# A hybrid attention and mixture-of-experts layer: its first projection summed in PSUM by eighths of the channels

## The chip, the cores and the metric

One core of a Trainium2 chip. The metric is the device time of one execution in microseconds (us), median of several runs. The program has some 27,500 instructions on five engines: PE (TensorE; PEld is its weight load), DVE (VectorE), ACT (ScalarE), POOL (GpSimd) and SP (SyncE, which issues nearly all DMAs).

## What is computed

256 tokens of 2048 channels go through one transformer layer in fp32. Only its beginning matters here: a normalized input is scaled and shifted by vectors that come from the conditioning vector `c`, and then multiplied by a wide matrix whose columns are the queries, keys and values of an attention, the inputs of a gated delta rule (`qb, kb, vb`, and its gate `zb`), and further gates.

```python
mod = (jax.nn.silu(c) @ w_ada + b_ada)[:, None, :]
sh1, sc1, g1, sh2, sc2, g2 = jnp.split(mod, 6, axis=-1)
u = layer_norm(x) * (1.0 + sc1) + sh1
hcat = u @ w_in
qa, ka, va, qb, kb, vb, zb, b_logit, a_logit, ga_logit, gb_logit = jnp.split(hcat, split_points, axis=-1)
oa = swa_sink_attention(qa, ka, va, swa_sinks)
...
merged = jax.nn.sigmoid(ga_logit) * (oa @ w_proj_a) + jax.nn.sigmoid(gb_logit) * (ob @ w_proj_b)
x = layer_norm(DEEPNORM_ALPHA * x + g1 * (merged @ w_out), ln1_g, ln1_b)
```

After that come a second scale and shift, a router and 32 experts.

## The kernel before, in words

**Data.** Channels lie on the 128 partitions: `xT` is the normalized input turned, 16 blocks `k` of 128 channels by 256 tokens. Weights come from memory in tiles of 1 MB (128x2048), one DMA on SP's queue each, into a rotating pool of four (`wp`, `wload`, L75). fp32 products are made from three reduced-precision ones: the weight tile is split by halves of 1024 columns into `wh` (cast on ACT, L275) and `wl` (the rest, DVE, L276), `u` into `uh` and `ul` (L176, L177), and `mm3` (L279) issues `wh*uh`, `wh*ul`, `wl*uh` (L280 to L282). One half of a weight tile is a **job**: 8 blocks of 128x128, so 24 products of 256 columns on PE.

**First stage.** Before `u` exists, its scale and shift must be computed from 32 tiles of `w_a01`, four for each of eight groups: quarter `q` of the channels, first scale (`i` = 1), then shift (0). In `first_mods` each tile gives four matmuls (L192) that stand side by side in 32 columns of PE each, into the bank `fa`; after four tiles ACT copies the bank (`fr`, L199), PE turns it by four transposes (`fc`, L169), DVE reduces it to four columns of scale or shift (L170, L171), and after the shift four blocks of `xT` become `u`, `uh`, `ul` (L175 to L177). I call this the turn of a quarter.

As soon as a quarter of `u` is there, its share of 20 column blocks (8 of queries, 2 of keys, 2 of values, 8 of `z`) is computed: `quarter` (L312) appends 10 jobs per quarter (`w_kq`, 5 tiles), each job giving two column blocks over four channel blocks in one PSUM bank `wq`. The first quarter's result is copied to SBUF by ACT (L334), those of the other three are added to it by DVE (L336). `run(few(mods, 8), QCH, ...)` weaves the scale-and-shift steps of the next quarter between the jobs.

**Main stream.** `pieces` appends jobs for the other columns: one tile of `w_in` is one column block over all 16 channel blocks (two jobs), summed in one bank `ws`. `run(chain, per, adas)` emits the jobs in order and puts between them `per` steps per job of a chain (a generator) and `adas` half tiles per job of the later modulation vectors (`ada_steps`, a DVE multiply-add per half tile, L220). The constants `PER` and `ADA` hold these rates for five stretches. The first stretch has the 12 blocks of `conv_todo(0)` (24 jobs) with the chain `gates`, `attn_v`, `attn`, `z_silu`; what is left of the chain when the jobs end is emitted behind them. Then come `conv_todo(1)` with the delta rule `gdn(0)`, the projections with `gdn(1)`, the output projection, and the experts.

**Order.** A scheduler fixes one static order for each engine from the program's order and the dependences; SP's queue is in order too. `sml` and `cmx`, constants that the gates need, are loaded behind the first stage (L801 to L803).

Of the kernel before, what the change touches and what calls it, by code (L numbers as in the profile page):

```python
# [9 lines left out]
F32 = mybir.dt.float32  # L10
# [6 lines left out]
P = 128  # L17
D = 2048
# [48 lines left out]
def tile_block(ctx: ExitStack, tc: tile.TileContext, A: dict, out: bass.AP, dbg=None, upto=99):  # L67
# [63 lines left out]
    SC.activation(csil, craw[:, 0:KT], AF.Silu)  # L131
    crep = gd.tile([P, KT, 32], F32, name="crep")
# [24 lines left out]
    def early_room():  # L157

        a = r1.tile([P, 1024 + 7 * 512], F32, tag="G1", name="wx0")
        b = r2.tile([P, KT, S], F32, tag="X1", name="wx1").rearrange("p k s -> p (k s)")  # L160
        return [t[:, 2048 * j:2048 * j + 2048] for t in (a, b) for j in range(2)]

    def first_mods():

        def use(i, q, mr):
            dst = (sh1c, sc1c)[i][:, 4 * q:4 * q + 4]
            p = pg(f"fc{i}{q}")
            for m in range(4):
                T.transpose(p[:, m * P:(m + 1) * P], mr[:, m * P:(m + 1) * P], ident)  # L169
            V.tensor_reduce(dst, p.rearrange("p (m j r) -> p m j r", m=4, j=4)[:, :, :, 0], axis=AX.X, op=ADD)  # L170
            V.scalar_tensor_tensor(dst, dst, float(i), craw[:, KT * (i + 1) + 4 * q:KT * (i + 1) + 4 * q + 4],  # L171
                                   op0=ADD, op1=ADD)
            if i == 0:
                for k in range(4 * q, 4 * q + 4):
                    V.tensor_scalar(xT[:, k, :], xT[:, k, :], sc1c[:, k:k + 1], sh1c[:, k:k + 1], op0=MUL, op1=ADD)  # L175
                    SC.copy(uh[:, k, :], xT[:, k, :])  # L176
                    V.tensor_tensor(ul[:, k, :], xT[:, k, :], uh[:, k, :].bitcast(F32), op=SUB)  # L177

        late = []
        room = early_room()  # L180
        for q in range(4):
            for i in (1, 0):
                pa = pg(f"fa{i}{q}")
                for t in range(4):
                    src = A["w_a01"][(4 * i + q) * 4 + t]
                    if room:
                        w = room.pop(0)
                        nc.sync.dma_start(w, src)
                    else:
                        w = wload(src)  # L190
                    for k in range(4):
                        T.matmul(pa[32 * k:32 * k + 32, :], crep[:, 4 * t + k, :], w[:, 512 * k:512 * k + 512],  # L192
                                 start=(t == 0), stop=(t == 3))
                    if late and t == LT[1 - i]:
                        use(*late.pop())
                    if t < 3:
                        yield
                mr = rb.tile([P, 512], F32, tag="mr", name=f"fr{i}{q}")
                SC.copy(mr, pa)  # L199
                if i == 0 and LT[0] < 0:  # L200
                    use(i, q, mr)
                else:
                    late.append((i, q, mr))
                yield
        if late:
            use(*late.pop())
        yield
# [44 lines left out]
    sh1c = gd.tile([P, KT], F32, name="sh1c")  # L252
    sc1c = gd.tile([P, KT], F32, name="sc1c")
# [4 lines left out]
    mods = first_mods()  # L258
    for _ in range(FM):
        next(mods)  # L260
    for t in range(NT):
        x0 = xx[:, t, :]
        mu, rs = ln_stats(x0, f"a{t}")
        V.tensor_scalar(x0, x0, mu, rs, op0=SUB, op1=MUL)
        for kq in range(4):
            p = pg(f"xt{t}{kq}")
# [45 lines left out]
    def quarter(q, dsts):  # L312

        for t in range(len(dsts) // 4):
            st = {}

            def prep(hf, t=t, st=st):
                if hf == 0:
                    st["w"] = wload(A["w_kq"][q * TQ + t])
                return split(st["w"][:, hf * 1024:(hf + 1) * 1024])  # L320

            def fin(sp, hf, t=t):
                h, lo = sp
                p = ps_w.tile([P, 512], F32, tag="ws", name=f"wq{q}{t}{hf}")
                for m in range(2):
                    for k in range(4):
                        kk = slice(k * 256 + m * P, k * 256 + m * P + P)
                        mm3(p[:, m * S:(m + 1) * S], (h[:, kk], lo[:, kk]), (uh[:, 4 * q + k, :], ul[:, 4 * q + k, :]),
                            k == 0, k == 3)
                        if k % 2 and m + k < 4:  # L330
                            yield
                dst = dsts[4 * t + 2 * hf].rearrange("p m s -> p (m s)")
                if q == 0:
                    SC.copy(dst, p)  # L334
                else:
                    V.tensor_tensor(dst, dst, p, op=ADD)  # L336

            for hf in range(2):
                jobs.append((lambda hf=hf, prep=prep: prep(hf), lambda sp, hf=hf, fin=fin: fin(sp, hf)))
# [439 lines left out]
    def few(it, n):  # L779
        for _ in range(n):  # L780
            next(it, None)
            yield

    a0 = r2.tile([P, KT, S], F32, tag="X1", name="a0")
# [7 lines left out]
    dsts = [a0[:, i:i + 2, :] for i in range(11)] + [None] + [szT[:, i:i + 2, :] for i in range(7)] + [None]  # L792
    for _ in range(8 - FM + (LT[0] >= 0)):
        next(mods)
    for q in range(4):
        quarter(q, dsts)
    for q in range(3):
        run(few(mods, 8), QCH, split_at=2 * TQ)
    for _ in mods:
        pass  # L800
    for dst, n in ((sml, "small"), (cmx, "cmx")):  # L801
        V.tensor_copy(dst[:, 0:1], sh1c[:, 0:1])
        nc.sync.dma_start(dst, A[n])  # L803
    pieces(conv_todo(0))
    run(None, split_at=2 * TQ)
# [681 lines left out]
def pack(inp):  # L1487
# [6 lines left out]
    a01 = ada[:, :2 * D].reshape(4, 4, P, 2, 4, 512)  # L1494
    r["w_a01"] = a01.transpose(3, 4, 0, 2, 1, 5).reshape(32, P, D)
# [15 lines left out]
    n = 4 * TQ  # L1511
    r["w_kq"] = w[:, cols[:n * P]].reshape(4, 4, P, TQ, 2, 256).transpose(0, 3, 2, 4, 1, 5).reshape(n, P, D)
# [52 lines left out]
```

## Time and profile before

| | |
|---|---|
| median of 3 runs | 1822.61 us (1822.32 to 1824.35) |
| the profiled execution, its own time | 1820.14 us |
| its span, first to last instruction | 1818.2 us |
| mean granted clock of TensorE, of full speed | 0.985 |
| busy over the span: PE, DVE, ACT | 95%, 49%, 28% |
| DMA | 628.59 MB, mean 346 GB/s |

The profile gives for each group of instructions its line, engine, output and inputs, count, busy time and mean duration, and the idle time of the engine just before it with what ended it. A matmul of fp32 data has two records in the trace (two passes). A busy PE is not PE at its peak, since matmuls overlap: the pace is read from starts, or from a stretch's time over its count.

### The profile page before, as it was taken

The page shows a single profiled execution, that of the slowest core. Times are in us where ns is not written, and L with a number is a line of the kernel's source. Part 1 is how long each engine was busy: PE and PEld are TensorE (multiplying, and loading weights), DVE is VectorE, ACT ScalarE, POOL GpSimd, SP SyncE. Part 2 cuts the span into 40 slices and gives each one's busy share as a digit, 9 for nine tenths or more (in the row PEclk, how much of TensorE's full clock was granted, in tenths as well). Part 3 has the DMA queues.
Part 4 walks back from the last instruction along what each step waited for, and adds up shares of the span by engine and source line. Part 5 has one row for each costly group of instructions (what it writes and reads, how often), then busy time and mean ns, then how long its engine had stood idle before and what let it go on. Part 6 is the DMA issues. An engine that isn't in the chain of part 4 may idle for free. (4 is left out here: it accounts for less than half of the span.)

```text
span 1818.2 us, 27495 instructions
## 1 busy us (share of the span) xinstructions
PE 1724.2 (95%) x11518; PEld 1108.4 (61%) x11518; DVE 899.9 (49%) x1463; ACT 516.7 (28%) x957; POOL 45.2 (2%) x49
## 2 busy tenths in 40 slices
PE   5999998999999999998999999999999999999995
PEld 3778987898999999885434443444434444343331
DVE  3345897888878878667123321232123322232026
ACT  3423698336333544435101110011101110011101
POOL 1000000203000000000000000000000000000000
PEclk9999999999999999998999999999999999999998
DMA  9887566465778688978999999999999999999995
GB/s 365 326 320 305 216 240 224 169 242 217 265 288 297 241 302 303 373 283 325 368 380 421 420 420 421 421 420 420 420 421 420 420 421 420 420 420 421 401 423 231
DMA packets 87289, 628.59 MB, mean 346 GB/s; under 512 B 9829, under 2 KB 9829, under 8 KB 11253
## 3 DMA queue, kind: packets, MB, share of 16 engines
q1 hardware_dynamic: 86832, 626.43, 86.4%
q8 instruction: 92, 1.51, 0.3%
q10 hardware_dynamic: 328, 0.36, 0.1%
q14 instruction: 37, 0.30, 0.0%
HBM read 624.65 MB, written 2.10 MB: 345 GB/s over the span
## 5 line engine op out<-in xcount | busy, mean ns | idle before, releaser
L275 ACT CAST wh<-w 128x1024 fp32r<-128x1024 f32 x216 | 226.0, 1049 | 323.4 <-PE ws L281 115.9
L276 DVE TENSOR_TENSOR wl<-w,wh 128x1024 fp32r<-128x1024 f32 x216 | 266.0, 1232 | 77.1 <-PE mx L281 22.8
L1223 PE MATMUL pg<-w,XT 128*64 128x512 f32 x1024 | 277.8, 598 | 3.9 <-DMA w<-in_w_gu 2.9
L1223 PE MATMUL pu<-w,XT 128*64 128x512 f32 x1024 | 274.6, 592 | 0.0
L280 PE MATMUL ws<-uh,wh 128*128 128x256 f32 x896 | 259.8, 290 | 1.1 <-ACT wh L275 1.1
L282 PE MATMUL ws<-uh,wl 128*128 128x256 f32 x896 | 254.6, 284 | 1.9 <-DVE wl L276 1.6
L281 PE MATMUL ws<-ul,wh 128*128 128x256 f32 x896 | 253.9, 283 | 0.0
L1261 PE MATMUL pd<-w,hT 128*64 128x512 f32 x1016 | 234.1, 599 | 0.8 <-DVE hT L1238 0.8
L1230 DVE TENSOR_TENSOR hs<-hs,pu 128x512 f32<-128x512 f32 x16 | 11.0, 688 | 429.0 <-PE pu L1223 429.0
L280 PEld LDWEIGHTS ws<-uh,wh 128*128 128x128 f32 x896 | 169.7, 189 | 11.3 <-issue 7.8
L282 PEld LDWEIGHTS ws<-uh,wl 128*128 128x128 f32 x896 | 169.9, 190 | 3.8 <-DVE wl L276 2.9
L281 PEld LDWEIGHTS ws<-ul,wh 128*128 128x128 f32 x896 | 169.9, 190 | 1.0 <-issue 0.8
L1223 PEld LDWEIGHTS pu<-w,XT 128*64 128x64 f32 x1024 | 77.6, 137 | 146.2 <-issue 146.2
L220 DVE SCALAR_TENSOR_TENSOR acc<-w,csil,acc 128x1024 f32<-128x1024 f32 x128 | 163.1, 1290 | 6.3 <-DMA w<-in_w_ada 6.2
L1223 PEld LDWEIGHTS pg<-w,XT 128*64 128x64 f32 x1024 | 72.5, 136 | 133.9 <-issue 113.1
L1202 PEld LDWEIGHTS xg<-G,xh 128*128 128x128 f32 x1024 | 120.3, 193 | 41.0 <-issue 25.8
L1261 PEld LDWEIGHTS pd<-w,hT 128*64 128x64 f32 x1016 | 66.4, 136 | 124.1 <-issue 110.3
L1202 PE MATMUL xg<-G,xh 128*128 128x128 f32 x1024 | 131.7, 283 | 6.7 <-DVE x L1278 3.5
L1229 ACT ACTIVATE hs<-pg 128x512 f32<-128x512 f32 x16 | 9.6, 597 | 438.9 <-PE pg L1223 438.9
L370 ACT CAST dh<-pd 128x512 fp32r<-128x512 f32 x64 | 37.5, 586 | 281.4 <-DVE pd L1264 161.1
L1264 DVE SCALAR_TENSOR_TENSOR pd<-pd,wsl,g2b 128x512 f32<-128x512 f32 x64 | 48.5, 758 | 103.7 <-PE pd L1261 103.7
L280 PE MATMUL wq<-uh,wh 128*128 128x256 f32 x320 | 93.1, 294 | 5.1 <-ACT uh L176 2.7
(374 smaller groups left out, 2264.4 us busy)
## 6 DMA issues: line engine op xcount, KB each, us to landing
w<-in_w_gu SPq DMA_DIRECT2D x256, 1024.0 KB, 19.8
w<-in_w_dn SPq DMA_DIRECT2D x127, 1024.0 KB, 19.8
w<-in_w_ada SPq DMA_DIRECT2D x64, 1024.0 KB, 5.1
w<-in_w_in SPq DMA_DIRECT2D x56, 1024.0 KB, 4.8
w<-in_w_a SPq DMA_DIRECT2D x28, 1024.0 KB, 6.7
w<-in_w_kq SPq DMA_DIRECT2D x20, 1024.0 KB, 7.0
w<-in_w_pab SPq DMA_DIRECT2D x16, 1024.0 KB, 4.9
w<-in_w_out SPq DMA_DIRECT2D x16, 1024.0 KB, 6.1
```

The lines of the kernel that those rows point to most:

```text
L220: V.scalar_tensor_tensor(acc[:, hc], w[:, hc], csil[:, k:k + 1], acc[:, hc], op0=MUL, op1=ADD)
L275: SC.copy(h, w)
L276: V.tensor_tensor(lo, w, h.bitcast(F32), op=SUB)
L280: T.matmul(p, a[0], b[0], start=first, stop=False)
L281: T.matmul(p, a[0], b[1], start=False, stop=False)
L282: T.matmul(p, a[1], b[0], start=False, stop=last)
L370: SC.copy(h, src)
L1202: T.matmul(p[:, k * P:(k + 1) * P], xh[t][:, (4 * kq + k) * P:(4 * kq + k + 1) * P], Gs[t].bitcast(F32), start=(t == 0), stop=(t == NT - 1))
L1223: T.matmul(dst[64 * e:64 * e + 64, :], XT[:, k, 64 * e:64 * e + 64], we[:, e * 1024 + hv * 512:e * 1024 + hv * 512 + 512], start=(k == 0), ...
L1230: V.tensor_tensor(hs, hs, pup, op=MUL)
L1261: T.matmul(pd[64 * e:64 * e + 64, :], hT[:, f, 64 * e:64 * e + 64], we[:, (2 * (f % 2) + e) * 512:(2 * (f % 2) + e + 1) * 512], start=(f = ...
L1264: V.scalar_tensor_tensor(pd, pd, ws, g2b[:, cs], op0=MUL, op1=MUL)
```

## The change

The first stage goes by eighths of the channels instead of quarters, and covers 12 column blocks (queries, keys, values) instead of 20. For an eighth, scale and shift (two channel blocks each) lie in one bank, so four tiles of `w_a01` and one turn give both. The 12 column blocks have their sums in six PSUM banks for the whole stage (`acc`, two blocks to a bank); the banks are first written by one matmul of zeros each, every product then adds, and each bank is copied out once at the end (three by ACT, three by DVE). The jobs of the stage are 24 (three per eighth), and the steps of the next eighth are written between them by hand. The loads go through ten places (two halves each of three buffers that are needed later, and the four of `wp`), where before four such places were used once each. The 8 blocks of `z` become 16 jobs of the main stream, ahead of `conv_todo(0)`, so that this stretch has 40 jobs. `PER` and `ADA` are set anew. The PSUM pools of the main stream are opened after the first stage, with waits tile by tile. The packing of weights on the host follows.

```diff
-PER = (1.66, 1.55, 0.85, 2.0)
-ADA = (0.9, 0.9, 1.05, 0.63, 0.09)
+FQ = 12
+PER = (1.0, 1.55, 0.85, 2.0)
+ADA = (0.8, 0.9, 0.95, 0.6, 0.09)
...
+    ps_f = fps.enter_context(tc.tile_pool(name="ps_f", bufs=2, space=PSUM))
+    ps_q = fps.enter_context(tc.tile_pool(name="ps_q", bufs=FQ // 2, space=PSUM))
...
+    def stage_buffers():
+
+        g = r1.tile([P, 1024 + 7 * 512], F32, tag="G1", name="wx0")
+        a = r2.tile([P, KT, S], F32, tag="X1", name="wx1").rearrange("p k s -> p (k s)")
+        most = [t[:, 2048 * j:2048 * j + 2048] for t in (g, a) for j in range(2)] + [None] * 4
+        yield from most
+        x2 = r2.tile([P, KT, S], F32, tag="X2", name="wx2").rearrange("p k s -> p (k s)")
+        while True:
+            yield from [x2[:, 0:2048], x2[:, 2048:4096]] + most
...
+    def mod_rows(e, t):
+
+        if t == 0:
+            fa[e] = ps_f.tile([P, 512], F32, tag="f", name=f"fa{e}")
+        w = sload(A["w_a01"][4 * e + t])
+        for k in range(4):
+            T.matmul(fa[e][32 * k:32 * k + 32, :], crep[:, 4 * t + k, :], w[:, 512 * k:512 * k + 512],
+                     start=(t == 0), stop=(t == 3))
+        if t == 3:
+            mr = rb.tile([P, 512], F32, tag="mr", name=f"fr{e}")
+            SC.copy(mr, fa[e])
+            fa[e] = mr
...
+    def mod_turn(e):
+
+        mr = fa.pop(e)
+        p = ps_f.tile([P, 512], F32, tag="f", name=f"fc{e}")
+        for m in range(4):
+            T.transpose(p[:, m * P:(m + 1) * P], mr[:, m * P:(m + 1) * P], ident)
+        dst = modc[:, :, 2 * e:2 * e + 2]
+        V.tensor_reduce(dst, p.rearrange("p (i m j r) -> p i m j r", i=2, m=2, j=4)[:, :, :, :, 0], axis=AX.X, op=ADD)
+        V.tensor_tensor(dst, dst, craw[:, KT:].rearrange("p (i k) -> p i k", i=2)[:, :, 2 * e:2 * e + 2], op=ADD)
+        for k in range(2 * e, 2 * e + 2):
+            V.tensor_scalar(xT[:, k, :], xT[:, k, :], sc1c[:, k:k + 1], sh1c[:, k:k + 1], op0=MUL, op1=ADD)
+            SC.copy(uh[:, k, :], xT[:, k, :])
+            V.tensor_tensor(ul[:, k, :], xT[:, k, :], uh[:, k, :].bitcast(F32), op=SUB)
...
+    def by_eighths():
+
+        acc = [ps_q.tile([P, 512], F32, tag="q", name=f"wq{j}") for j in range(FQ // 2)]
+        for p in acc:
+            T.matmul(p, zero, zero[:, 0:1].to_broadcast([P, 512]), start=True, stop=False)
...
+        mod_turn(0)
+        sp = prep(0)
+        for n in range(24):
+            e, b = n // 3 + 1, n % 3
+            if b < 2 and e < 8:
+                mod_rows(e, 2 * b)
+                mod_rows(e, 2 * b + 1)
+            cur, sp = sp, (prep(n + 1) if n < 23 else None)
+            for i, _ in enumerate(products(n, cur)):
+                if b == 1 and i == 1 and e < 8:
+                    mod_turn(e)
...
-    for q in range(4):
-        quarter(q, dsts)
-    for q in range(3):
-        run(few(mods, 8), QCH, split_at=2 * TQ)
...
+    pieces([(FQ + m, lambda ps, m=m: SC.copy(szT[:, m, :], ps)) for m in range(8)])
     pieces(conv_todo(0))
-    run(None, split_at=2 * TQ)
     ch = seq(gates(), attn_v(), attn(), z_silu())
     run(ch, PER[0], ADA[0])
```

Three places show how the built programs' order moves. First PE at the start of the stage, from the turned input (`xt`) to the first products `wq`; `fa` are the scale-and-shift matmuls, `fc` the transposes of a turn. Before:

```order
L268 MATMUL xt_185<-cst,xx 128x128 x4
L192 MATMUL fa_110<-wx_109,crep 32x512 x8
L192 MATMUL fa_212<-w,crep 32x512 x4
L169 MATMUL fc_219<-cst,fr_210 128x128 x4
L192 MATMUL fa_212<-w,crep 32x512 x12
L169 MATMUL fc_246<-cst,fr_244 128x128 x4
L280 MATMUL wq_275<-uh,wh 128x256
```

And with the change:

```order
L263 MATMUL xt_196<-cst,xx 128x128 x4
L311 MATMUL wq_209<-zero 128x512
L311 MATMUL wq_210<-zero 128x512
L186 MATMUL fa_107<-wx_109,crep 32x512 x4
L311 MATMUL wq_211<-zero 128x512
L311 MATMUL wq_212<-zero 128x512
L311 MATMUL wq_213<-zero 128x512
L311 MATMUL wq_214<-zero 128x512
L198 MATMUL fc_221<-cst,fr_130 128x128 x4
L186 MATMUL fa_240<-w,crep 32x512 x4
L275 MATMUL wq_209<-uh,wh 128x256
```

The first products stood behind eight tiles of `w_a01` and two turns; now they stand behind five tiles, six matmuls of zeros and one turn, four of the zeros between the last tile and the turn.

Then PE at a later turn, `fa` being the last tiles of the group. Before (the second quarter):

```order
L282 MATMUL wq_602<-uh,wl 128x256
L192 MATMUL fa_507<-w,crep 32x512 x8
L169 MATMUL fc_642<-cst,fr_640 128x128 x4
L280 MATMUL wq_665<-uh,wh 128x256
L280 MATMUL wq_697<-uh,wh 128x256
L281 MATMUL wq_665<-ul,wh 128x256
```

With the change (the fourth eighth; `wq_209` is the bank that the next eighth's first products write):

```order
L186 MATMUL fa_489<-wx_287,crep 32x512 x4
L277 MATMUL wq_212<-uh,wl 128x256
L186 MATMUL fa_489<-wx_287,crep 32x512 x4
L198 MATMUL fc_559<-cst,fr_540 128x128 x4
L275 MATMUL wq_213<-uh,wh 128x256
...
L277 MATMUL wq_214<-uh,wl 128x256
L186 MATMUL fa_612<-wx_108,crep 32x512 x4
L275 MATMUL wq_209<-uh,wh 128x256
```

Before, the products behind a turn were those of the new quarter; now 24 products of the old eighth (`wq_213`, `wq_214`) stand between a turn and the first product that needs its result. In four of the seven later turns the last tile stands right before the transposes, as here; in three it stands seven products earlier.

Last, SP's queue at the end of the stage. Before:

```order
L77 DMA w<-in_w_a 128x2048 x2
L803 DMA sml<-in_small 128x641
L803 DMA cmx<-in_cmx 128x1104
L77 DMA w<-in_w_kq 128x2048 x4
L77 DMA w<-in_w_in 128x2048 x2
```

With the change (`wx` are the added places, `w` the four of the pool):

```order
L74 DMA w<-in_w_kq 128x2048
L171 DMA wx_287<-in_w_a 128x2048 x2
L171 DMA wx_108<-in_w_a 128x2048 x2
L171 DMA wx_109<-in_w_kq 128x2048 x2
L799 DMA sml<-in_small 128x641
L799 DMA cmx<-in_cmx 128x1104
L74 DMA w<-in_w_in 128x2048 x2
```

The last six tiles of the stage need no place of the pool, so the first tiles for `z` stand right behind the constants.

## Rows read from the trace of the kernel before

**Rows 1.** Busy time by stretch (us from the start; x is the count).

```profile
core 0: us, PE busy (x) PEld busy (x) DVE busy (x) ACT busy (x) POOL busy (x), PEclk, DMA share, GB/s
22.00:28.00 6.00, 3.68 (x28) 0.79 (x27) 0.34 (x2) 0.28 (x1) 0.00 (x0) 1.00 1.00 418
28.00:34.00 6.00, 1.72 (x12) 0.58 (x12) 2.08 (x9) 1.88 (x4) 0.00 (x0) 0.94 1.01 418
34.00:40.00 6.00, 5.42 (x23) 5.13 (x24) 3.46 (x7) 2.88 (x6) 0.00 (x0) 0.50 0.94 360
...
34.00:193.60 159.60, 153.60 (x1203) 126.89 (x1204) 80.58 (x113) 58.24 (x77) 0.00 (x0) 0.97 0.80 306
193.60:291.70 98.10, 94.23 (x752) 86.08 (x751) 89.69 (x168) 83.30 (x204) 0.91 (x3) 1.00 0.63 230
291.70:327.50 35.80, 30.29 (x276) 26.82 (x274) 27.41 (x39) 29.64 (x84) 6.26 (x4) 0.90 0.57 212
...
640.00:680.00 40.00, 40.00 (x339) 40.00 (x338) 33.17 (x38) 17.62 (x23) 0.00 (x0) 1.00 0.83 304
820.00:830.00 10.00, 10.00 (x46) 8.29 (x45) 9.58 (x9) 3.16 (x3) 0.00 (x0) 1.00 0.77 281
120.00:140.00 20.00, 19.92 (x143) 16.47 (x144) 9.24 (x14) 6.04 (x8) 0.00 (x0) 0.91 0.72 278
...
70.00:80.00 10.00, 7.91 (x59) 5.48 (x59) 5.17 (x11) 5.92 (x10) 0.00 (x0) 1.00 0.86 342
```

**Rows 2.** Groups of PE's instructions from 34 to 193.6 us.

```profile
line engine op names shapes xcount | busy us, mean ns | idle before us <-releasers
L280 PE MATMUL wq<-uh,wh 128*128 128x256 f32 x320 | 93.1, 294 | 5.1 <-ACT uh L176 2.7 <-ACT wh L275 2.4
...
L192 PE MATMUL fa<-w,crep 128*32 128x512 f32 x192 | 25.4, 604 | 0.5 <-DMA w<-in_w_a 0.5
L169 PE MATMUL fc<-cst,fr 128*128 128x128 f32 x24 | 3.9, 286 | 2.1 <-ACT fr L199 2.1
L392 PE MATMUL ba<-xT,sml 128*32 128x256 f32 x26 | 2.1, 387 | 0.0
```

**Rows 3.** Timeline of the start (start, duration, what; idle before).

```profile
19.70 1.92 PE L192 MATMUL fa<-wx,crep 128*32 128x512 f32 x16
...
22.90 0.66 PE L169 MATMUL fc<-cst,fr 128*128 128x128 f32 x4
...
24.29 1.06 PE L192 MATMUL fa<-w,crep 128*32 128x512 f32 x8 [0.74 <-DMA w<-in_w_a]
...
29.26 1.07 PE L192 MATMUL fa<-w,crep 128*32 128x512 f32 x8 [1.42 <-DMA w<-in_w_a]
...
31.78 0.17 DVE L170 TENSOR_REDUCE sh1c<-fc 128x4 f32<-128x16 f32 x1 [7.82 <-PE fc L169]
...
32.71 0.40 ACT L176 CAST uh<-xT 128x256 fp32r<-128x256 f32 x1 [1.67 <-DVE xT L175]
33.02 1.04 ACT L275 CAST wh<-w 128x1024 fp32r<-128x1024 f32 x1
...
34.11 0.58 PE L280 MATMUL wq<-uh,wh 128*128 128x256 f32 x1 [2.37 <-ACT wh L275]
```

**Rows 4.** Timeline of the second quarter's turn on PE.

```profile
76.09 0.66 PE L169 MATMUL fc<-cst,fr 128*128 128x128 f32 x4 [0.70 <-ACT fr L199]
78.10 0.51 PE L280 MATMUL wq<-uh,wh 128*128 128x256 f32 x2 [1.35 <-ACT uh L176]
```

**Rows 5.** Instructions that read the bank `wq` (duration min/median/max, first and last start).

```profile
L336 DVE TENSOR_TENSOR a<-a,wq x18: 686/689/690, 82.5 to 182.4; 128x512 f32<-128x512 f32 x18
L336 DVE TENSOR_TENSOR szT<-szT,wq x12: 680/687/691, 105.4 to 194.4; 128x512 f32<-128x512 f32 x12
```

**Rows 6.** What PE waited for, 180 to 340 us (total, times, longest).

```profile
PE pb L749 <- ACT PT L743: 3.5, 2, 3.3
...
PE ws L282 <- DVE wl L276: 1.6, 3, 0.8
```

More of the change, by code (lines that the diff above doesn't have):

```diff
@@ L131, in tile_block @@
     SC.activation(csil, craw[:, 0:KT], AF.Silu)
+    zero = gd.tile([P, P], F32, name="zero")
+    G.memset(zero, 0.0)
     crep = gd.tile([P, KT, 32], F32, name="crep")
@@ L155, in ada_tile @@
         return wload(A["w_ada"][k * P:(k + 1) * P, (i - 2) * D:(i - 1) * D])
[L157 to L180, printed above, removed]
-        for q in range(4):
[L182 to L207, printed above, removed]
@@ new lines, in sload @@
+    def sload(src):
+        w = next(room)
+        if w is None:
+            return wload(src)
+        nc.sync.dma_start(w, src)
+        return w
+    modc = gd.tile([P, 2, KT], F32, name="modc")
+    sh1c, sc1c = modc[:, 0, :], modc[:, 1, :]
+    V.tensor_scalar(craw[:, 2 * KT:], craw[:, 2 * KT:], 1.0, None, op0=ADD)
+    fa = {}
+    def mod_rows(e, t):
[9 more added lines that the diff above has]
+            fa[e] = mr
@@ L257, in tile_block @@
     nc.sync.dma_start(xx[:, 1, :], A["x"][P:2 * P, :])
-    mods = first_mods()
-    for _ in range(FM):
-        next(mods)
+    for t in range(4):
+        mod_rows(0, t)
     for t in range(NT):
@@ L265, in tile_block @@
         for kq in range(4):
-            p = pg(f"xt{t}{kq}")
+            p = ps_q.tile([P, 512], F32, tag="q", name=f"xt{t}{kq}")
             for k in range(4):
@@ L310, in pieces @@
                 jobs.append((lambda hf=hf, prep=prep: prep(hf), lambda sp, hf=hf, fin=fin: fin(sp, hf)))
[L312 to L339, printed above, removed]
@@ new lines, in by_eighths, with prep, products @@
+    def by_eighths():
+        acc = [ps_q.tile([P, 512], F32, tag="q", name=f"wq{j}") for j in range(FQ // 2)]
+        for p in acc:
+            T.matmul(p, zero, zero[:, 0:1].to_broadcast([P, 512]), start=True, stop=False)
+        ld = {}
+        def prep(n):
+            if n % 2 == 0:
+                ld["w"] = sload(A["w_kq"][n // 2])
+            return split(ld["w"][:, (n % 2) * 1024:(n % 2 + 1) * 1024])
+        def products(n, sp):
+            h, lo = sp
+            e, b = n // 3, n % 3
+            for pc in range(4):
+                m = 4 * b + pc
+                for k in range(2):
+                    kk = slice(k * 512 + pc * P, k * 512 + pc * P + P)
+                    mm3(acc[m // 2][:, (m % 2) * S:(m % 2 + 1) * S], (h[:, kk], lo[:, kk]),
+                        (uh[:, 2 * e + k, :], ul[:, 2 * e + k, :]), False, (e, k, m % 2) == (7, 1, 1))
+                if pc < 3:
+                    yield
+        mod_turn(0)
[9 more added lines that the diff above has]
+                    mod_turn(e)
+        dst = r2.tile([P, KT, S], F32, tag="X1", name="a0")
+        for j, p in enumerate(acc):
+            d = dst[:, 2 * j:2 * j + 2, :].rearrange("p m s -> p (m s)")
+            if j % 2:
+                V.tensor_copy(d, p)
+            else:
+                SC.copy(d, p)
+        return dst
@@ L777, in seq @@
             yield from x
[L779 to L784, printed above, removed]
+    a0 = by_eighths()
     at["q"], at["k"], at["v"] = a0[:, 0:8, :], a0[:, 8:10, :], a0[:, 12:14, :]
@@ L803, in tile_block @@
         nc.sync.dma_start(dst, A[n])
+    fps.close()
+    pps = ExitStack()
+    ps_w = pps.enter_context(tc.tile_pool(name="ps_w", bufs=2, space=PSUM, reuse_waits="tile"))
+    ps_a = pps.enter_context(tc.tile_pool(name="ps_a", bufs=1, space=PSUM, reuse_waits="tile"))
+    ps_g = pps.enter_context(tc.tile_pool(name="ps_g", bufs=5, space=PSUM, reuse_waits="tile"))
+    pieces([(FQ + m, lambda ps, m=m: SC.copy(szT[:, m, :], ps)) for m in range(8)])
     pieces(conv_todo(0))
-    run(None, split_at=2 * TQ)
     ch = seq(gates(), attn_v(), attn(), z_silu())
```

30 lines of the change are left out of this document (8 added, 22 removed).

## The prediction

> **What bounds the kernel now.** I read the busy time by stretch first, to see which engine each stage leans on. From 34.0 to 193.6 us, the products of the first stage, PE is busy 153.6 of 159.6 us, DVE 80.6, ACT 58.2, and the DMA engines at 0.80 of their time [rows 1]. So PE sets the pace there, and work taken off DVE or ACT buys nothing by itself. What does PE do with the time? Its pace with nothing in the way is read where PE, at the full clock, runs little but products: 339 in 40 us, 118 ns each, so a job of 24 products is 2.83 us [rows 1]. The 960 products of the stage are then 113.3 us. The tiles of the next scale and shift add 25.4, the transposes 3.9, the gates' first matmuls 2.1 [rows 2]: 144.7. The other 14.9 us are lost, and the columns on the right say where: waits for `uh`, `wh` and `fr` [rows 2], which stand at the turns of the quarters (0.70 before the transposes, 1.35 behind them [rows 4]), and stretches at a lower clock, 0.50 of full speed from 34 to 40 us and a mean of 0.91 from 120 to 140 [rows 1].
>
> Then the start. Until 34.1 us not one product runs. The timeline shows PE reading one tile of scale and shift every 2.49 us (from 24.29 to 29.26, two steps), each wait ended by a DMA [rows 3], while the DMA engines are full (1.00 and 1.01, 418 GB/s [rows 1]). So the start is bound by the loads that stand ahead of the first product: two of the input and eight of `w_a01`.
>
> Last, the stretch behind the stage, where the attention runs beside 24 jobs: all three engines are nearly full from 193.6 to 291.7 (PE 94.2, DVE 89.7, ACT 83.3 of 98.1), and in the tail PE idles 5.5 of 35.8 us at a mean clock of 0.90 [rows 1].
>
> **The change part by part.** I count to one place that both kernels have: all 40 jobs of queries, keys, values and `z` done. Before, that is 193.6 us.
>
> *The start.* The fourth tile's matmuls end at 19.70 + 1.92 = 21.6 as before, since six loads stand ahead in both. Behind them come four matmuls of zeros. The trace has none; two tiles, each with the same 512 columns in two passes, take 1.92, so 0.96 each [rows 3], 3.8 together, which I take because PE is at the full clock from 22 on [rows 1]; at half of it they would be 7.7, and at nothing the turn could come 3.8 earlier. The copy `fr` hides behind them. Transposes 0.66, then from DVE's reduction to the end of the first `uh` 32.71 + 0.40 - 31.78 = 1.33 [rows 3]. The first product comes at 21.6 + 3.8 + 0.66 + 1.33 = 27.4 instead of 34.1. Before, it waited for `wh` instead, whose cast stood behind `uh` on ACT [rows 3]; now the cast stands ahead.
>
> *The stage.* 576 products at 118 ns: 68.0. 28 tiles at 25.4 / 24 = 1.06: 29.7. Seven transposes at 0.66: 4.6. In four of the seven turns the last tile stands right before the transposes, so the wait for `fr` stays, 0.70 each: 2.8. The wait of 1.35 behind a turn should mostly go, since 24 products (2.83 us) of the old eighth stand there: `uh` needs 1.33 of it. But the second block's `ul` queues behind a cast of `wh` (1.04) and its DVE partner, so I keep 0.5 a turn (between 0 and 1.35): 3.5. Sum 108.6, so the stage ends at 136.0.
>
> Could the loads hold it up? The tile read at 29.26 is the tenth load of the queue. The last but one of the 46 loads of the stage is then there at 29.26 + 35 x 2.49 = 116.4, and its cast (1.04) and four jobs (11.3) end at 128.8. That is the floor of the stage; per eighth the loads need 5.5 x 2.49 = 13.7 us against PE's (108.6 - 8.5) / 7 = 14.3. With ten places they can run ahead by 25 us; nothing on SP's queue waits for a place that is not long free.
>
> *`z` in the main stream.* 384 products at 118 ns are 45.3; their copies on ACT and casts lie beside. The gates' 2.1 us move behind the stage. The place is reached at 136.0 + 45.3 + 2.1 = 183.4 instead of 193.6: **10.2 us gained**.
>
> *DVE and ACT.* 30 additions of 0.69 [rows 5], 20.6 us of DVE, go; six copies come. Cost and gain nothing, as DVE idles half of that stage [rows 1]; without that cover it would be worth up to 20. The end copies are hidden too, since `z` sums in other banks.
>
> *The attention's stretch.* The same chain, 40 steps at 1.0 over 40 jobs instead of 39.8 at 1.66 over 24, so the tail of steps behind the jobs stays the same. DVE gets 16 splits (1.2 each) and 10.4 more half tiles (1.3 each), 33 us, over 45 more: 123 of 143, less crowded than before. What PE can get back is its idle 3.9 us, and at most some of the tail's 5.5. Of the named waits in there 1.6 are for `wl` and 3.5 for the attention's own copies [rows 6]. I take **4 us**, between 0 and 9.
>
> *Later.* `ADA`, over the jobs of the five stretches, brings 40 x 0.8 + 24 x 0.9 + 48 x 0.95 + 48 x 0.6 + 32 x 0.09 = 130.9 of 132 half tiles, where 24 x 0.9 + 24 x 0.9 + 48 x 1.05 + 48 x 0.63 + 32 x 0.09 = 126.7 came before: four fewer at the end, some 5 us of DVE, where PE is full (10.0 of 10 from 820 on [rows 1]). Nothing, at most 2. The experts follow unchanged.
>
> Sum: 14.2 us off the profiled execution's own 1820.1 gives 1805.9. The median of the runs shown is 2.5 above that execution, so I predict **1808.5**.
>
> **The rivals.** *The loads set the pace and PE loses nothing beside them:* the stage ends at its floor, 128.8, 7.2 earlier: 1801.3. For it: 13.7 against 14.3 us an eighth is close, and PE could run on at the full clock. Against: the waits at the turns are in PE's own order.
>
> *The turns cost as much as before:* seven at 0.70 + 1.35 instead of 6.3 in all are 8.1 more, and with the zeros at half clock 3.9 more still: 1816.6 to 1820.5. For it: a turn's chain through ACT, PE and DVE is as long as it was, and there are seven instead of three. Against: the 24 products behind each.
>
> *The clock falls at each eighth (slower):* PE now meets seven turns and 28 tiles that may come just in time. After waits of 1.4 us per tile and 2.4 at the turn [rows 3], the clock stood at 0.50 from 34 to 40, where 23 products took 6.0 instead of 2.7 us [rows 1]: 3.3 lost. One fall an eighth, seven times, is 23.1 on top of the forecast: 1808.5 + 23.1 = 1831.6. It decides from five falls on (16.5 is more than the gain). For it: the clock fell again between 120 and 140, behind the third quarter's turn. Against: from 22 to 28, busy 3.68 of 6, it stayed at 1.00, and so it did from 70 to 80 [rows 1], where a turn with 2.05 us of waits stands [rows 4]. The Trainium skill speaks against the change here: "TensorE: Matmul & The Clock Gate", section "Loop structure matters more than you think", calls a loop bad whose matmuls wait for a transfer each round, as PE then runs at its lower clock. By that rule the result would be this rival's; the trace agrees at 34 us and not at 22.
>
> *The change does less than it says:* the gain is given back by the attention's stretch, whose chain might be as late as before. Then about 1822. Little speaks for it: its inputs come earlier and the jobs beside it are those that PE needs anyway.
>
> **How the numbers follow.** A measurement of this kernel can tell 0.2% (3.6 us) from no change. Chances: the forecast 0.60 (1803 to 1814 with the bounds of the zeros, turns and relief), loads at the floor 0.20 (1796 to 1803), turns as dear as before 0.12, falling clock 0.06, given back 0.02. Faster by over 0.2%, below 1819.0: the first two and half of the third, 0.86. Within 0.2%: the other half and the last, 0.08. Slower 0.06. The range from 1799 to 1819 leaves out the lower end of the second (some 0.07), half of the third and the last two: 0.21.
>
> **What would show it.** First product near 27.4 us, last of the bank `wq` near 136, and no DVE addition on it; the DMA engines near 1.00 of their time until 118 us; waits at a turn of about 1 us on PE; no clock below full speed from 28 to 136; `z` and gates done near 183; the attention's stretch with less idle PE and then everything earlier by the same amount. The forecast is wrong if the stage ends beyond 146, if the clock falls in it more than once, or if the tail of the attention grows.

## The result, and the profile after

The change made the kernel slower: 1840.83 us (median of 4 runs, 1835.03 to 1865.54) against 1822.46 for the kernel before. One of the four runs, 1865.54 with a mean clock of 0.931, was disturbed; the ratio, 1.0088 with a 95% interval of 1.0063 to 1.0113, is that of the other three (median 1839.95). The forecast was 1808.5 in a range of 1799 to 1819, so the sign was wrong. The profiled execution took 1835.03, its span 1833.2 at a mean clock of 0.983; the sum had made 1805.9 of it. The difference to be explained is 29.1 us.

The lines of the changed kernel: L186 is the tiles' matmul (`fa`), L190 the copy `fr`, L198 the transposes `fc`, L200 to L205 the turn on DVE and ACT (`uh` is L204), L270 and L271 the casts `wh` and `wl`, L275 to L277 the products, L311 the zeros.

First the start. PE's and ACT's rows until the first product:

```profile
20.80 1.89 PE L311 MATMUL wq<-zero 128*128 128x512 f32 x4
22.62 1.07 PE L186 MATMUL fa<-wx,crep 128*32 128x512 f32 x8
23.61 3.71 PE L311 MATMUL wq<-zero 128*128 128x512 f32 x8
27.16 0.60 PE L198 MATMUL fc<-cst,fr 128*128 128x128 f32 x4
...
29.17 0.75 PE L275 MATMUL wq<-uh,wh 128*128 128x256 f32 x4 [0.41 <-ACT uh L204]
...
23.75 0.59 ACT L190 COPY fr<-fa 128x512 f32<-128x512 f32 x1 [2.06 <-PE fa L186]
```

Here the prediction held in kind: the first product comes at 29.2 (27.4 forecast, 34.1 before [rows 3]). All six zeros were on PE's path, not four, and they delayed the last tile too.

Then the stage. Busy time by stretch, the last row being the 40 jobs that follow it:

```profile
core 0: us, PE busy (x) PEld busy (x) DVE busy (x) ACT busy (x) POOL busy (x), PEclk, DMA share, GB/s
34.00:60.00 26.00, 22.42 (x162) 16.06 (x161) 6.64 (x10) 5.77 (x8) 0.00 (x0) 0.93 1.01 420
60.00:80.00 20.00, 15.14 (x101) 9.43 (x99) 6.50 (x14) 5.38 (x9) 0.00 (x0) 0.91 1.02 422
...
100.00:120.00 20.00, 16.38 (x99) 10.86 (x98) 6.44 (x11) 4.92 (x7) 0.00 (x0) 0.80 0.81 299
120.00:140.00 20.00, 18.25 (x132) 13.16 (x135) 6.64 (x10) 4.24 (x6) 0.00 (x0) 0.93 0.89 355
140.00:160.00 20.00, 16.73 (x101) 12.06 (x94) 4.58 (x9) 6.05 (x9) 2.77 (x9) 0.76 0.16 57
168.20:316.00 147.80, 141.60 (x1173) 133.26 (x1171) 125.20 (x198) 108.21 (x252) 0.92 (x3) 1.00 0.69 255
```

The last product of the bank `wq` starts at 168.1 instead of the forecast 136. No row from 34 to 160 us has the full clock, where the forecast said none would be below it; and PE idles up to 4.9 us of 20. The loads are not to blame: they run ahead and are nearly done at 140 (DMA share 0.16 from there). What PE waited for from 20 to 168.2 us (total, times, longest):

```profile
PE wq L275 <- ACT wh L270: 13.0, 7, 2.5
PE fc L198 <- ACT fr L190: 3.0, 4, 0.8
PE wq L277 <- DVE wl L271: 2.6, 5, 0.5
PE wq L275 <- ACT uh L204: 0.4, 1, 0.4
```

19.0 us, and the largest is a wait that the prediction did not have: `wh`, seven times, once at each turn. The first turn, in the rows of PE, of ACT and of DVE, shows why:

```profile
37.44 1.06 PE L186 MATMUL fa<-wx,crep 128*32 128x512 f32 x8
39.26 0.66 PE L198 MATMUL fc<-cst,fr 128*128 128x128 f32 x4 [0.76 <-ACT fr L190]
42.21 0.39 PE L275 MATMUL wq<-uh,wh 128*128 128x256 f32 x1 [2.29 <-ACT wh L270]
...
43.47 0.40 PE L277 MATMUL wq<-uh,wl 128*128 128x256 f32 x1 [0.52 <-DVE wl L271]
...
38.62 0.59 ACT L190 COPY fr<-fa 128x512 f32<-128x512 f32 x1 [9.20 <-PE fa L186]
40.81 0.40 ACT L204 CAST uh<-xT 128x256 fp32r<-128x256 f32 x1 [1.60 <-DVE xT L203]
41.12 1.04 ACT L270 CAST wh<-wx 128x1024 fp32r<-128x1024 f32 x1
42.07 0.40 ACT L204 CAST uh<-xT 128x256 fp32r<-128x256 f32 x1
...
40.37 0.73 DVE L203 TENSOR_SCALAR xT<-xT,modc 128x256 f32<-128x256 f32 x2
```

The 24 products behind the transposes do belong to the old eighth, and their `u` has long been there. But their weights have not been cast: on ACT the cast `wh` for them (41.12) stands behind `fr` and the first `uh` of the turn itself. Its tile, the second of `w_kq`, had landed at 35.5 by the record of its DMA, and ACT idled 9.20 us before `fr` and 1.60 before `uh`, while the cover waited. So PE waits 0.76, runs four transposes, and waits 2.29 and 0.52 more. The other odd turns look like this one (the fifth and the seventh without the wait for `wl`). At the three even turns not 24 but nine products of the old eighth stand behind the transposes; then PE waits 1.23 for the `wh` of the next eighth's first job, and 0.53 for its `wl`. So the 24 products that the section on the change counts behind a turn are there at four of the seven later turns. The second turn on PE, and the cast on ACT:

```profile
59.75 0.62 PE L198 MATMUL fc<-cst,fr 128*128 128x128 f32 x4
...
62.66 0.39 PE L275 MATMUL wq<-uh,wh 128*128 128x256 f32 x1 [1.23 <-ACT wh L270]
...
61.57 1.04 ACT L270 CAST wh<-w 128x1024 fp32r<-128x1024 f32 x1
```

What follows such a wait, in stretches cut at the clock's changes:

```profile
36.00:42.20 6.20, 3.16 (x25) 1.88 (x24) 1.50 (x6) 1.98 (x4) 0.00 (x0) 1.00 1.01 423
...
43.70:47.10 3.40, 3.40 (x18) 3.40 (x18) 1.19 (x2) 0.66 (x1) 0.00 (x0) 0.50 1.01 422
```

For 3.4 us after the turn the granted clock is 0.50, that is 1.2 instead of 2.4 GHz. The same comes behind all seven turns: at 43.7, 64.2, 81.3, 101.7 and 139.3 for 3.4 us each, at 115.4 and 152.9 for 6.8. That is 30.6 us at half clock, which costs half of it, 15.3.

In the 40 jobs of `z` and the attention's stretch, 168.2 to 316.0, the clock is full, and the named waits are

```profile
PE ws L277 <- DVE wl L271: 4.9, 7, 1.0
PE ws L275 <- ACT wh L270: 1.2, 1, 1.2
```

where the 24 jobs before had 1.6 for `wl` [rows 6]. The place at which the two kernels stand alike (start of `conv_todo(1)`) is reached at 316.0 instead of 291.7, 24.3 late; the end is 15.0 late (1833.2 against 1818.2), so 9.3 come back on the way.

### The profile page after: what moved, and what is told of

Same layout as the page of the kernel before. It is cut to its first block, busy times and chain, and to the rows that moved or that the text cites. A ratio compares the mean times of both kernels' runs of the same rounds, so it can differ in the third digit from the quotient of the medians.

```text
span 1833.2 us, 27471 instructions
## 1 busy us (share of the span) xinstructions
PE 1733.7 (95%) x11530; PEld 1112.2 (61%) x11530; DVE 885.2 (48%) x1437; ACT 513.1 (28%) x957; POOL 43.2 (2%) x50
## 5 line engine op out<-in xcount | busy, mean ns | idle before, releaser
L277 PE MATMUL ws<-uh,wl 128*128 128x256 f32 x1024 | 291.3, 284 | 8.2 <-DVE wl L271 8.2
L275 PE MATMUL ws<-uh,wh 128*128 128x256 f32 x1024 | 296.6, 290 | 1.2 <-ACT wh L270 1.2
L271 DVE TENSOR_TENSOR wl<-w,wh 128x1024 fp32r<-128x1024 f32 x202 | 249.6, 1237 | 89.5 <-PE mx L276 24.3
L276 PE MATMUL ws<-ul,wh 128*128 128x256 f32 x1024 | 290.0, 283 | 0.0
L270 ACT CAST wh<-w 128x1024 fp32r<-128x1024 f32 x202 | 210.6, 1048 | 260.4 <-PE ws L276 108.4
L275 PEld LDWEIGHTS ws<-uh,wh 128*128 128x128 f32 x1024 | 194.3, 190 | 11.8 <-issue 8.8
L277 PEld LDWEIGHTS ws<-uh,wl 128*128 128x128 f32 x1024 | 194.2, 190 | 11.1 <-DVE wl L271 10.8
L276 PEld LDWEIGHTS ws<-ul,wh 128*128 128x128 f32 x1024 | 194.4, 190 | 0.4 <-issue 0.3
L218 DVE SCALAR_TENSOR_TENSOR acc<-w,csil,acc 128x1024 f32<-128x1024 f32 x128 | 163.8, 1293 | 10.6 <-DMA w<-in_w_ada 10.6
L1279 DVE TENSOR_TENSOR x<-x,cb 128x512 f32<-128x512 f32 x120 | 76.9, 681 | 22.7 <-PE cb L1275 22.7
```

What stands on the lines that cost most here:

```text
L218: V.scalar_tensor_tensor(acc[:, hc], w[:, hc], csil[:, k:k + 1], acc[:, hc], op0=MUL, op1=ADD)
L270: SC.copy(h, w)
L271: V.tensor_tensor(lo, w, h.bitcast(F32), op=SUB)
L275: T.matmul(p, a[0], b[0], start=first, stop=False)
L276: T.matmul(p, a[0], b[1], start=False, stop=False)
L277: T.matmul(p, a[1], b[0], start=False, stop=last)
```

## The experiments

Two theories about the stage. **Order on ACT:** the covering products wait because their cast stands behind the turn in ACT's static order, and the clock falls because of these waits; mend the order and both go. **Loads or clock by themselves:** the eighths are too fine for the loads, or the clock would fall at each tile and turn whatever the order. And about the stretch behind it: was the relief eaten by DVE, by the chain's rate, or was it never there?

The stage in five of the kernels (start of the first product behind it, one of `z`; PE's named waits, in us, from 20 us on or, for e1 and e2, from the first product; us at half clock up to its end):

| kernel | time, us | ratio to before (95%) | stage ends | waits | half clock |
|---|---|---|---|---|---|
| the change | 1839.95 | 1.0088 (1.0063 to 1.0113) | 168.2 | 19.0 | 30.6 |
| e1, filled | 1824.93 | 1.0029 (1.0014 to 1.0044) | 155.2 | 6.6 | 6.8 |
| e2, tiles one ahead | 1828.49 | 1.0042 (1.0022 to 1.0063) | 156.8 | 16.9 | 10.2 |
| e4, order pinned | 1805.23 | 0.9906 (0.9890 to 0.9923) | 133.9 | 5.3 | 0 |
| e7, zeros spread | 1804.59 | 0.9905 (0.9887 to 0.9923) | 134.1 | 6.1 | 0 |

**e1: dummy products in the gaps.** At four of the seven turns three matmuls of zeros with 512 columns are added onto banks of the sums, one behind the last tile (it runs while PE waits for `fr`) and two behind the transposes, so that PE has work where it waited.

```diff
+    def fill(e, src, n):
+        for j in range(n if e % 2 else 0):
+            T.matmul(banks[j], zero, src[:, 0:512], start=False, stop=False)
...
+            fill(e, w, 1)
...
+        fill(e, mr, 2)
```

> The changed kernel with three matmuls more at each of the four odd turns (1, 3, 5, 7) of the first stage: zeros times data that the turn already holds, added to a sum bank (so the result stays), one behind the last tile of the eighth and two behind the transposes. They keep PE busy where it waits 0.76, 2.30 and 0.52 us in the changed kernel, and take 0.93 each. Theory (each wait of over a microsecond at a turn is followed by a fall of the clock, which costs about as much again): no fall near the odd turns, 20 us less at half clock in the first stage, 10 to 14 us less time than the changed kernel's 1835.0: 1821 to 1825. Rival (the waits alone cost, the falls are beside the point): only 4 x (3.6 - 2.8) = 3 us less, 1832. Rival (the loads or the adding into banks set the pace): no change, 1835.

The stage ended 13.0 us earlier although 12 matmuls were added to it, and the time, 1824.93, lies where it was expected. The two falls that are left (from 94.8 and 128.9 us) stand behind the fourth and the sixth turn, which got no dummies; behind the second, with the same waits of 1.23 and 0.52, there was none. Named waits (the lines are six higher in this kernel) and the dummies' groups:

```profile
PE wq L281 <- ACT wh L276: 3.7, 3, 1.2
PE wq L283 <- DVE wl L277: 2.5, 7, 0.5
...
```

```profile
L182 PE MATMUL wq<-fr,zero 128*128 128x512 f32 x16 | 7.5, 593 | 0.0
L182 PE MATMUL wq<-wx,zero 128*128 128x512 f32 x8 | 4.5, 644 | 0.0
```

The dummies were busy 12.0 us, about what the waits shrank by (19.0 to 6.6): idle time was replaced by useless work. What was gained on top is the clock: half of 30.6 - 6.8 is 11.9, and 13.0 was measured. So the falls are a consequence of PE's gaps at the turns and cost what half clock says. In this build ACT's order at the odd turns moved as well (`wh` ahead of `uh`), so the shrinking of the waits is not the dummies' doing alone; how much of it is theirs stays open.

**e2: the weight tiles loaded one ahead.** In the change the next `w_kq` tile is asked for when its job is prepared, which puts it behind the last `w_a01` tile of the eighth. Here it is asked for one job earlier.

```diff
-            if n % 2 == 0:
-                ld["w"] = sload(A["w_kq"][n // 2])
-            return split(ld["w"][:, (n % 2) * 1024:(n % 2 + 1) * 1024])
+            return split(ld[n // 2][:, (n % 2) * 1024:(n % 2 + 1) * 1024])
...
+            if n % 2 == 0:
+                get(n // 2 + 1)
```

> The changed kernel with each weight tile of the stage loaded one job earlier, ahead of the scale-and-shift tiles of that job. On ACT the casts (wh) of the jobs around a turn then stand ahead of the copy and the casts that belong to the turn, at all seven later turns. Theory (at a turn PE waits for a cast of wh that stands on ACT behind the turn's own uh, 13.0 us in all, and the clock falls after it): the waits for wh go, the seven or so waits for fr of 0.76 stay, at most two falls are left; the first stage ends at 138 to 146 instead of 167.8 and the time is 1808 to 1816. Rival (the loads or the adding into banks set the pace): the stage ends at 160 or later, 1828 or more. Rival (the turn's own chain through ACT, PE and DVE sets the pace): half of the waits come back as waits for uh or ul, 1820 to 1828.

```profile
PE wq L275 <- ACT uh L204: 10.9, 8, 1.4
PE fc L198 <- ACT fr L190: 5.4, 7, 1.1
PE wq L277 <- DVE wl L271: 0.6, 2, 0.3
```

The wait for `wh` is gone, and another has its place: the scheduler now put each turn behind all products of the old eighth, so nothing covers it, and `fr` and `uh` are waited for at every turn. The expected end at 138 to 146 us did not come: of 19.0 us of waits 16.9 are back on `uh`, `fr` and `wl`, as the expectation's last rival had it (its 1820 to 1828 was 0.5 short). This is also the prediction's rival "the turns cost as much as before". It is worth 11.4 us against the change all the same: 2.1 of waits and half of 20.4 us of clock, 10.2. With waits of some 2.1 us a turn ((10.9 - 1.4 + 5.4) / 7, without the one at the start) the clock fell three times in seven turns (at 78.6, 95.7 and 146.9), not behind each, and not behind the fifth, which waited longest, 2.69.

**e3: the kernel before with only `z` moved.** Quarters as before, 12 column blocks instead of 20 in the stage, `z` as 16 jobs of the main stream, the rates of the change.

```diff
-TQ = 5
-QCH = 0.73
+TQ = 3
+QCH = 1.34
...
-    dsts = [a0[:, i:i + 2, :] for i in range(11)] + [None] + [szT[:, i:i + 2, :] for i in range(7)] + [None]
+    dsts = [a0[:, i:i + 2, :] for i in range(11)] + [None]
...
+    pieces([(4 * TQ + m, lambda ps, m=m: SC.copy(szT[:, m, :], ps)) for m in range(8)])
```

> The kernel before with one part of the change alone: the first stage keeps its quarters, its two banks and DVE's additions, but covers 12 column blocks (three tiles per quarter), and the 8 blocks of z are jobs of the main stream ahead of the first convolution blocks, with the changed kernel's rates. Theory (what the change loses it loses at the seven turns of the first stage; moving z is neutral within what the loads allow): 1816 to 1828. Rival (z in the main stream costs, since it makes the attention's stretch longer without relieving it): 1830 or more.

1824.76 us, a ratio of 1.0025 (1.0007 to 1.0042): moving `z` alone is no gain and costs a little (3.2 us by the medians, 1824.76 against 1821.53; 1.3 to 7.7 by the interval), inside the expected 1816 to 1828. The stage and the 40 jobs:

```profile
34.50:155.00 120.50, 111.58 (x818) 80.33 (x819) 53.58 (x84) 39.26 (x56) 0.00 (x0) 0.96 0.87 334
155.10:304.60 149.50, 143.63 (x1146) 135.31 (x1145) 124.33 (x197) 108.06 (x251) 0.92 (x3) 0.98 0.69 254
```

24 jobs of the stage with their tiles take 120.5 us; with 45.3 for `z` that is 165.8 where the stage before took 159.5 (34.1 to 193.6). PE idles 8.9 us of the 120.5, and idled 6.0 of the longer stage before [rows 1]: the tiles and turns are covered less. The 40 jobs take 149.5, of which a fall of 6.8 us at half clock is 3.4: the same stretch as in the change, with the old stage ahead of it. So what that stretch takes does not come from the eighths.

**e4: PE's order pinned.** On top of e2, each block of PE's work in the stage is tied behind the one before it in the program. The order of an eighth is then: two tiles, job one, two tiles, half of job two, transposes `fc`, the other half and job three (36 products), next eighth.

```diff
+        def after(fn, *args):
+            with tc.issue_after(pe[-1].ins):
+                fn(*args)
...
-                mod_rows(e, 2 * b)
-                mod_rows(e, 2 * b + 1)
+                after(mod_rows, e, 2 * b)
+                after(mod_rows, e, 2 * b + 1)
             cur, sp = sp, (prep(n + 1) if n < 23 else None)
-            for i, _ in enumerate(products(n, cur)):
+            it = products(n, cur)
+            for i in range(4):
+                after(next, it, None)
                 if b == 1 and i == 1 and e < 8:
-                    mod_turn(e)
+                    after(mod_turn, e)
```

> Edit on e2 (kq tiles loaded one ahead): TensorE's order in the stage is pinned to the program's order. In each eighth the last two tiles of the next eighth's modulation run ahead of the middle job, the turn's transposes stand behind half of that job, and its other half and the third job (36 products, 4.3 us) stand behind the transposes and ahead of the next eighth; on ScalarE the cast wh of the third job now stands ahead of fr and uh. The order on ScalarE is the cause (our theory): the waits of 19 us in the stage fall to 3 to 6 us, most falls of the clock go with them (under 10 us at half clock in the stage instead of 30.6), the last wq product is at 134 to 141 instead of 168, and the time is 1803 to 1814 us, under both kernels. Rival 1, the loads pace the stage, or the products behind a turn need something else late (uh of the other channel, wl): the end of the stage stays at 150 or later, time 1819 or more. Rival 2, the clock falls at the eighths for another reason than the waits: waits go but 20 us or more at half clock stay, end of the stage at 145 to 150, time 1814 to 1820.

Busy time by stretch, all of PE's named waits of the stage, and ACT's rows around the first turn:

```profile
34.00:60.00 26.00, 23.37 (x191) 17.05 (x188) 10.28 (x18) 8.10 (x12) 0.00 (x0) 1.00 1.01 420
...
100.00:120.00 20.00, 19.04 (x159) 14.03 (x156) 6.64 (x10) 6.00 (x8) 1.45 (x6) 1.00 1.01 418
120.00:133.90 13.90, 13.90 (x120) 13.90 (x119) 8.76 (x13) 8.58 (x13) 1.13 (x4) 1.00 0.79 325
133.90:281.60 147.70, 142.24 (x1172) 133.36 (x1171) 124.75 (x198) 108.53 (x252) 0.92 (x3) 1.00 0.69 256
```

```profile
PE fa L186 <- DMA w<-in_w_a: 4.2, 5, 1.4
PE fa L186 <- DMA wx<-in_w_a: 1.1, 1, 1.1
```

```profile
24.08 2.94 ACT L270 CAST wh<-w 128x1024 fp32r<-128x1024 f32 x3
...
33.37 1.05 ACT L270 CAST wh<-w 128x1024 fp32r<-128x1024 f32 x1 [4.10 <-PE wq L276]
36.58 0.59 ACT L190 COPY fr<-fa 128x512 f32<-128x512 f32 x1 [2.16 <-PE fa L186]
39.46 0.73 ACT L204 CAST uh<-xT 128x256 fp32r<-128x256 f32 x2 [2.29 <-DVE xT L203]
```

The casts of all three jobs of the first eighth, that of the covering one among them, are done from 24.08 on, and that of the next eighth's first job (33.37) stands ahead of `fr` too. No wait on ACT or DVE is left in the stage; the only ones are for tiles of `w_a01`, with the DMA engines at 1.01 of their time until 120. The clock is full throughout. The stage ends at 133.9, the time is 1805.23: 17 us under the kernel before and 35 under the change. Both rivals of the expectation fall: the loads bound the stage, but at 134, and the clock does not fall at tiles and turns as such.

**e5 and e6: the stretch behind the stage.** Each is e4 with one rate changed: e5 takes the chain at the old rate, e6 leaves 12 half tiles of the later modulation for later.

```diff
-PER = (1.0, 1.55, 0.85, 2.0)
+PER = (1.66, 1.55, 0.85, 2.0)
```

> e4 with one number changed: the rate at which the chain (gates, attention) is taken in the 40 jobs that follow the stage goes back from 1.0 to 1.66 a job, so that its work lies in some 24 jobs and the other 16 stand nearly alone. Theory that a product beside the chain's work costs some 10 ns more, and that this is why the stretch of 40 jobs took 147.8 us instead of the forecast 141.5: the stretch gets 2 to 4 us shorter than in e4 (pure products in 16 jobs). Rival, the excess comes with the products themselves or with VectorE's additions for the modulation, whatever the chain does: the stretch stays within 1 us, or gets longer. Time within 4 us of e4 either way.

```diff
-ADA = (0.8, 0.9, 0.95, 0.6, 0.09)
+ADA = (0.5, 0.9, 0.95, 0.6, 0.09)
```

> e4 with one number changed: the modulation's multiply-adds on VectorE in the 40 jobs that follow the stage go from 0.8 to 0.5 a job (12 of 1.28 us leave the stretch, 15 us of VectorE's 125). Theory that VectorE's load delays wl (waits L277 on wl of 4.9 us in the change) and so ate the relief: the stretch gets 3 to 5 us shorter than in e4, the 12 come later and the end of the kernel gains 0 to 3 us or loses up to 5 if they land at the end. Rival, VectorE does not bound there: the stretch stays within 1 us and the end is 0 to 8 us later.

The 40 jobs, first of e5, then of e6:

```profile
134.20:290.40 156.20, 148.50 (x1198) 138.50 (x1197) 126.61 (x202) 110.80 (x260) 0.92 (x3) 0.98 0.65 236
```

```profile
134.20:283.90 149.70, 142.43 (x1173) 134.43 (x1171) 114.15 (x189) 109.26 (x253) 0.92 (x3) 0.99 0.58 211
```

Both expectations of a shorter stretch were wrong. e5's took 8.5 us longer than e4's 147.7 (two falls of the clock, waits for `PT` and `attP`), but no work of the chain was left behind the jobs, so four jobs later it was 1.6 behind, and its 1803.87 us cannot be told from e4's 1805.23. e6 relieved DVE by 10.6 us, yet the waits for `wl` were 5.9 us instead of 4.2 and the stretch 2.0 longer (one fall is 1.7 of that). Its 12 half tiles came back at the end: from the last product of `mx` to the first of `pg` it took 39.9 us instead of 31.1 (with 17.1 us at half clock instead of 10.2, some 3.4 of the difference), and the time is 1812.98. So DVE's load is not what stands in the way there.

**e7: the zeros spread.** e4 with two zeros ahead of the first turn, two behind its transposes, two behind three pieces of the first job.

```diff
-        for p in acc:
-            T.matmul(p, zero, zero[:, 0:1].to_broadcast([P, 512]), start=True, stop=False)
+        clear(acc[:2])
...
         mod_turn(0)
+        after(clear, acc[2:4])
...
+                if n == 0 and i == 2:
+                    after(clear, acc[4:])
```

> e4 with the six clearing products by zero spread: two where they were, two behind the first turn's transposes, two behind the first three pieces of the first job, so that the transposes fc no longer wait behind four of them (3.7 us in the change, with fr ready 2.8 us before fc ran). Theory that with the order pinned the loads pace the stage (e4's only waits of TensorE in it are 5.3 us for tiles of w_a, DMA at 420 GB/s): the first fc comes 2 to 3 us earlier, the waits for w_a grow by about as much, the last wq product stays within 1 us of e4's 133.8 and the time within 2 us of e4's. Rival, the start sets the end of the stage: it ends 2 to 3 us earlier and the time is 2 to 3 us under e4's 1805.

```profile
23.80 0.66 PE L198 MATMUL fc<-cst,fr 128*128 128x128 f32 x4 [0.71 <-ACT fr L190]
...
29.35 1.06 PE L186 MATMUL fa<-w,crep 128*32 128x512 f32 x8 [1.33 <-DMA w<-in_w_a]
30.34 0.39 PE L275 MATMUL wq<-uh,wh 128*128 128x256 f32 x1
```

The transposes run at 23.8 instead of behind the zeros, and PE waits for tiles in their stead: first product at 30.3 and end of the stage at 134.1, as in e4 (30.3 and 133.9), 1804.59 us. With the order mended, the loads pace the stage and the zeros are free.

## Why the prediction was wrong

Its sum for the stage was about right for a kernel whose covering products have their weights in time: e4, where they do, ends it at 133.9 against the forecast of 136.0. That e4's time, 1805.2, also lies near the forecast of 1808.5 is in part luck: the stretch behind the stage took 147.7 instead of 141.5, and behind that e4's profiled execution made up 6.1 us that the forecast did not have, 3.4 of them by the clock (see "Later"). Step by step:

- **What bounds the kernel.** PE paces the first stage, and work taken off DVE buys nothing: held. The 30 additions left DVE's rows, as said, and DVE and ACT idle more than half of the stage.
- **The start.** 29.2 instead of 27.4: +1.8. The zeros were rightly priced (0.96 each, 0.93 measured), but six lay on the path instead of four.
- **The turns: the step that failed.** "The wait of 1.35 behind a turn should mostly go, since 24 products (2.83 us) of the old eighth stand there", so 0.5 a turn and 6.3 us of waits in the stage. It asked whether the products had their `u`, and not whether they had their weights. The prediction even named "a cast of `wh`" in ACT's queue, as something that delays `ul`; that the same queue delays the cast was the point. At the three even turns, besides, nine products stood there and not 24. Measured: 19.0, of which 0.4 belongs to the start, and 13.0 for `wh` alone; that is +12.3. The Trainium skill has the rule, in "PSUM — Partial Sum Buffer", section "Engine vs sequencer instructions": the queues of ScalarE and VectorE are strictly first in, first out. The rows at 38.62 to 42.07 agree: a cast whose weights were there waited behind a copy and a `uh` that were not ready.
- **The clock: the rival at 0.06.** It gave 1831.6 from seven falls. They came, one behind each turn, together 30.6 us at half clock, +15.3. What spoke against it, that the second turn of the kernel before had 2.05 us of waits and no fall [rows 4], was one case: the third, with the same waits (0.70 at 118.03, 1.35 at 120.03), had a fall, as the prediction itself said, so 0.06 was low by its own rows. The waits of the odd turns were longer (0.76 + 2.29 + 0.52), but those of the even turns shorter, 1.75 in all, and the clock fell behind them too. So the size of a turn's waits does not decide alone, and what else does stays open. Its price of 3.3 a fall was that of one 6.8 us long; one of 3.4 costs 1.7. "TensorE: Matmul & The Clock Gate", section "Loop structure matters more than you think", in the Trainium skill, was right about the result and not about the way: its bad loop has a long wait for a transfer between every two matmuls, and here PE waited for no transfer in the stage, and for ScalarE or VectorE 2.46 us at the longest. In e4, where it does wait for transfers (up to 1.43 us), the clock stayed full.
- **The floor by the loads.** 128.8 was a fair bound: e4 and e7, paced by them, end at 133.9 and 134.1.
- These terms make 1.8 + 12.3 + 15.3 = 29.4 of the 32.2 us by which the stage ended late; 2.8 are not named by a row.
- **`z` and the attention's stretch.** 141.5 forecast (45.3 + 2.1 + 98.1 - 4), 147.8 measured, +6.3. PE's busy time was as forecast: 141.60, where 94.23 [rows 1] + 45.3 + 2.1 make 141.6, so `z` cost what it should. The miss is idle time. The relief of 4 was to come from the 3.9 us that PE idled there before; it idles 6.2 now, 2.3 more instead of 4 less, and its waits for `wl` are 4.9 instead of 1.6 [rows 6]. e5 and e6 show that neither the chain's rate nor less work on DVE buys it back. What delays `wl` stays open.
- **Later.** 9.3 us came back where the forecast had nothing. Some 6.8 of them are the clock. Behind this place the kernel before had 30.6 us at half clock (from 299.5, 330.2, 453.1 and 838.8 for 6.8 each, from 859.3 for 3.4), the change 17.0 (from 320.2, 350.9 and 473.8 for 3.4 each, from 852.7 for 6.8); the last 15 us of both are left out. The first 50 us behind the place, before and with the change:

```profile
291.70:341.70 50.00, 41.16 (x409) 36.80 (x408) 39.43 (x56) 32.39 (x88) 10.55 (x7) 0.86 0.54 202
316.00:366.00 50.00, 44.54 (x475) 39.60 (x474) 38.95 (x53) 29.32 (x69) 11.34 (x8) 0.93 0.41 146
```

  That is the luck of one execution: in e1, e2 and e4, whose edits all lie ahead of this place, it was 27.2, 30.6 and 23.8. Why the other 2.5 came back was not tried. Four half tiles fewer at the end may be part of it, since 12 more cost time there (e6); the forecast had named them and counted nothing for them.
- **The sum.** 32.2 + 6.3 - 9.3 = 29.2 of the 29.1 us between 1835.0 and 1805.9. The median, 1839.95, lies 4.9 above the profiled execution, not 2.5: the runs of the change differ by their clock (0.983 at 1835.03, 0.978 at 1841.71).

So both causes are shown: the order by e4 against e2, which differ in nothing else, and that the clock's falls follow PE's gaps by e1 and e4, where both went together. Which gaps bring a fall is not shown. And the idea of the change holds: eighths, with sums in PSUM, gain 0.9% once the order of PE is pinned.

## What to carry to other kernels

When products are put behind a step to cover its wait, look at everything that the cover itself needs, on every queue: an operand's cast that stands behind the covered step on an in-order engine makes the cover wait for what it should hide. The order of the engines that feed PE is to be read at each such place before a wait is priced, and pinned if a scheduler decides it. And a gap on PE has a second price, the half clock behind it, which here was nearly as large as the gaps themselves (15.3 to 19.0 us).

## What was not expected of the hardware

That a fall of the clock cannot be told from the size of a turn's waits. It fell behind every turn of the change, with 3.1 to 3.6 us of waits at the odd turns and 1.75 at the even ones; in e1 behind two of three even turns with the same 1.75; in e2 behind three of seven with 2.1 to 2.7, not behind the longest; and behind none in e4 and e7, with single waits up to 1.43. And how well useless products pay: the 12.0 us of matmuls by zero in e1 took no more than the waits that went (12.4), and half of the 23.8 us less at half clock came back.
